# Products of zeros ahead of every four sums of squares, and the modulation of the next k tile inside a_v for k 1 to 8

## The chip, the core and the metric

The kernel runs on one core of one Trainium2 chip. A core has five engines with a queue of their own each: TensorE (PE, matrix products; the profile shows its weight loads apart, as PEld), VectorE (DVE), ScalarE (ACT), GpSimd (POOL) and SyncE (SP, which issues the DMAs here). Each works its queue off in order and waits on semaphores for the others. The metric is the device time of one execution in microseconds (us).

## What is computed

A trunk of two layers over 256 latent tokens and 256 context tokens of width 2048, all in float32. What matters here is how a layer begins:

```python
shift, scale, gate = jnp.split(silu_c @ w_mod[l] + b_mod[l], 3, axis=-1)
shift_c, scale_c, gate_c = jnp.split(silu_cc @ w_mod[l] + b_mod[l], 3, axis=-1)
h = rmsnorm(x, g_pre[l]) * (1.0 + scale[:, None]) + shift[:, None]
h_c = rmsnorm(ctx, g_pre[l]) * (1.0 + scale_c) + shift_c
proj = h @ w_in[l]
proj_c = h_c @ w_in[l]
```

`rmsnorm` divides each token by the root of the mean of its 2048 squares. `proj` is split by columns into nine parts: a_u, a_v, a_g (a gated MLP), b_q, b_k, b_v, b_g (attention) and c_x, c_g (a Fourier mixer). The branches' outputs are joined, go through an output projection and a second rmsnorm, and are added to the stream.

## The kernel before

**Layout.** The 2048 channels are 16 k tiles of 128 partitions. Latent and context tokens stand side by side, 512 columns: `yo[k]` holds x (later other things), `hh[k]` and `hl[k]` the high and the low part of h. A product of two float32 matrices is made of three products of such parts (`mm3`, L405 to L408). A float32 product that isn't split (`ps_mod`, `ps_rs`) shows as two records in the trace.

**The order.** PE's queue is written out by hand for the whole kernel. While the first stage lasts (until k 14 of layer 0's loop, L626) the queues of DVE, ACT and SP are in the order of the code too; after it a scheduler orders these.

**The prologue** (L1132 to L1173). SP issues the 16 x tiles, 256 KB each, then two small tables, the modulation weights of k tile 0 (four loads of 512 KB, L167: tiles `mraw` twice, `macc`, `vv`), a projection weight (`raw`, L365), the modulation weights of k tile 1 (`mg`, `mgl`, `hh`/`hl`), a projection weight, and so on. For each x tile ACT squares it into one of seven `w2k` buffers (L1144), one of which the first small table holds meanwhile, and PE sums it over the partitions by a product with ones (L1147). The sum for tile k goes to 32 of the 128 columns of the array, by k % 4:

```python
c = slice(32 * (k % 4), 32 * (k % 4) + 32)
PE.matmul(sq[c], ones[:, 0:32], q, start=k < 4, stop=k >= KT - 4, tile_position=(0, 32 * (k % 4)))
```

`warm(ps, n)` (L448 to L451) puts n products of zeros (`wz`, bfloat16, 128 x 512) into a PSUM bank that nobody reads yet; ahead of each sum stands one. After the sums, copies on ACT, small products, a power on GpSimd and a broadcast give `rb0`, one over the root mean square of each token.

**The modulation of a k tile** (`mod_start`, L151 to L192) is 16 products of the 16 blocks of SiLU(c), SiLU(c_ctx) with 128 columns each of scale and shift, in four groups (`kg`), four column groups of 32 in each. The generator stops after each group, so the caller places the groups. Then DVE transposes the result (L175), a small product sums four quarters (`ps_modc`, L180), and DVE adds the bias (L189 to L192). Each group's weights are loaded when its products are put in the queue; a load waits for its buffer, which the products of the k tile two before have used.

**Layer 0's opening loop** (L598 to L660). For each k it accumulates a_v (four token tiles, `start_av`, 12 products) and the first three heads of a_u (`start_au`, three products a head). Meanwhile the modulation of tile k + 1 is computed (`mods_next`, all four groups, then `LOADS[k]` loads of projection weights into three `raw` buffers), and with it `h_next` makes hh, hl of k + 1: DVE multiplies (L484), ACT adds the shift and rounds (L488), DVE makes the low part (L493). `h_next` also splits `SPLITS[k]` projection weights into high and low (ACT L384, DVE L386), which frees their raw buffers. Where the four modulation groups stand on PE:

| k | order on PE |
| --- | --- |
| 0 | a_v, groups, products of zeros, a_u |
| 1, 2 (`k < MIDDLE`) | a_v, a_u head 0, groups, a_u head 1, modc; k 2 then a_u head 2 for k 0 to 2 |
| 3, 4 | half of a_v, groups, other half, modc, a_u |
| 5 to 15 (`k >= NEXT`) | groups, a_v, modc, a_u |

`W` (L332 to L401) streams the projection weights; `take` asks it for the next tile. After the loop the other parts of the projection follow as products over all 16 k tiles (`tunit`, `ps_t`).

Of the kernel before, what the change touches and what calls it, by code (L numbers as in the profile page):

```python
# [66 lines left out]
def trunk_kernel(ctx: ExitStack, tc: tile.TileContext, xT, xhalf, cT, wss, wsl, wmod, win, wout0, wout1, const, vec, rows,  # L67
# [9 lines left out]
    def sb(shape, dt, tag, bufs=1):  # L77
        cnt[0] += 1
        return pool.tile(shape, dt, tag=tag, bufs=bufs, name=f"{tag}_{cnt[0]}")

    def w2k(shape, dt=F32):
        return sb(shape, dt, "w2k", W2K)

    def mm_ps(name="mm"):
        cnt[0] += 1
        return psum.tile([P, 512], F32, tag="mm", bufs=6, name=f"ps_{name}_{cnt[0]}")

    def ms_ps(name="ms"):
        cnt[0] += 1
        return psum.tile([P, 512], F32, tag="ms", bufs=2, name=f"ps_{name}_{cnt[0]}")  # L90
# [29 lines left out]
    def cc(name):  # L120
        o, w = COFF[name]
        return cst[:, o - P:o - P + w]
# [154 lines left out]

    LOADS = [1, 1, 1, 2, 1, 1, 1, 1, 1, 0, 2, 0, 1, 1, 1, 0]
    SPLITS = [1, 1, 1, 2, 0, 1, 0, 2, 1, 1, 0, 2, 0, 1, 1, 1]
    MIDDLE, NEXT = 3, 5  # L280
    LOWC = 60
    YT = 3.0
    GATES = {4: 0}, {0: 1}, {0: 2, 14: 3}, {}
# [48 lines left out]
    class Stream:  # L332
# [64 lines left out]
        def next(self):  # L397
            self.fetch()
            pace()
            self.pos += 1  # L400
            return self.out[self.pos - 1]  # L401
# [3 lines left out]
    def mm3(ps, st, mv, start, stop):  # L405
        PE.matmul(ps, st[0], mv[0], start=start, stop=False)  # L406
        PE.matmul(ps, st[0], mv[1], start=False, stop=False)  # L407
        PE.matmul(ps, st[1], mv[0], start=False, stop=stop)  # L408

    def part(w, c):  # L410

        def of(t):
            if not isinstance(t, list):
                return t[:, c]
            n = t[0].shape[-1]
            return t[c.start // n][:, c.start % n:c.start % n + c.stop - c.start]

        return of(w[0]), of(w[1])
# [29 lines left out]
    def warm(ps, n):  # L448

        for _ in range(n):  # L450
            PE.matmul(ps, wz[:, 0:P], wz, start=True, stop=True)  # L451
# [16 lines left out]
    def h_of(l, k, sl):  # L468

        if l == 0:  # L470
            return hh[k][:, sl], hl[k][:, sl]
        s, a = sl.start // S, sl.start % S
        t, b = (hh, hl)[s][k], a + sl.stop - sl.start
        return t[:, a:b], t[:, S + a:S + b]

    def make_h(l, k, rb, streams, between=()):

        if streams[0] == 0:
            new_h(k)
        t = w2k([P, T])  # L480
        for s in streams:
            sl = slice(s * S, (s + 1) * S)
            rsl = slice((s - streams[0]) * S, (s - streams[0] + 1) * S)
            V.scalar_tensor_tensor(out=t[:, sl], in0=yo[k][:, sl], scalar=gs[l][:, k, s:s + 1],  # L484
                                   in1=rb[:, rsl], op0=ALU.mult, op1=ALU.mult)
        for s in streams:
            sl = slice(s * S, (s + 1) * S)
            first = A.activation(h_of(l, k, sl)[0], t[:, sl], AF.Identity, bias=sh[l][:, k, s:s + 1])  # L488
        next(iter(between), None)
        for s in streams:  # L490
            sl = slice(s * S, (s + 1) * S)
            hi, lo = h_of(l, k, sl)
            last = V.scalar_tensor_tensor(out=lo, in0=t[:, sl], scalar=sh[l][:, k, s:s + 1],  # L493
                                          in1=hi.bitcast(F32), op0=ALU.add, op1=ALU.subtract)
        return first, last
# [58 lines left out]
    def layer(l):  # L554
        last = l == 1
        n = S if last else T
        nt = n // P
# [11 lines left out]
        au = [mm_ps("au") for _ in range(2)] + [ms_ps("au") for _ in range(1 - l)]  # L569
# [3 lines left out]
        def take(k, which=(0,)):  # L573

            for i in which:
                if k % (2, 4, 8)[i] == 0:
                    ws_[i] = W.next()

        def start_av(k, ts):
            avw = ws_[0]  # L580
            c = slice((k % 2) * 512, (k % 2 + 1) * 512)
            for t in ts:
                sl = slice(t * P, (t + 1) * P)
                mm3(av[t], h_of(l, k, sl), part(avw, c), k == 0, k == KT - 1)
# [13 lines left out]
        if l == 0:  # L598
            for k in range(KT):
                m = mod_start(k + 1, 1) if k + 1 < KT else iter([None] * 4)  # L600

                def mods_next():
                    for _ in range(4):
                        next(m)
                    for _ in range(LOADS[k]):
                        W.load()

                def h_next():

                    todo = SPLITS[k]  # L610
                    if k + 1 < KT:
                        list(m)
                        e = W.emitting(512) if todo else iter(())
                        next(e, None)
                        make_h(0, k + 1, rb0, [0, 1], e)
                        list(e)
                        todo -= todo > 0
                    for _ in range(todo):
                        W.emit()

                if k % 2 == 0:
                    take(k)
                if k >= NEXT:
                    mods_next()
                    start_av(k, range(nt))
                    if k == KT - 2:  # L626
                        first_stage.close()
                    h_next()
                    if k >= KT - 2:
                        for _ in range(2):  # L630
                            with low(LAG), tc.issue_after(W.last.ins):
                                next(mods)
                    take(k, (1, 2))
                    start_au(k)
                elif k == 0:
                    start_av(0, range(nt))
                    mods_next()
                    warm(au[2], 3)
                    h_next()
                    warm(au[2], 6)  # L640
                    take(0, (1,))
                    start_au(0, (0, 1))
                elif k < MIDDLE:
                    start_av(k, range(nt))
                    take(k, (1,))
                    start_au(k, (0,))
                    mods_next()
                    start_au(k, (1,))
                    h_next()
                    if k == 2:  # L650
                        ws_[2] = W.next()
                        for i in range(k + 1):
                            start_au(i, (2,))
                else:
                    start_av(k, range(nt // 2))
                    mods_next()
                    start_av(k, range(nt // 2, nt))
                    h_next()
                    take(k, (1,))
                    start_au(k)  # L660
        for i, (k0, nk) in enumerate(blocks if l else ()):
            for k in range(k0, k0 + nk):
# [466 lines left out]
    with tc.manual_schedule(engines={EN.PE}):  # L1129

        first_stage.enter_context(tc.manual_schedule(engines={EN.DVE, EN.Activation, EN.SP}))
        DMA.dma_start(ct, cT)  # L1132
        for k in range(KT):
            DMA.dma_start(yo[k], xT[k])
        raw = w2k([P, NFIRST])
        DMA.dma_start(raw, const[:, 0:NFIRST])
        DMA.dma_start(vecs, vec)
        V.memset(wz, 0.0)
        A.activation(cs, ct, AF.Silu)
        V.tensor_copy(cpad[:, :, 0:2], cs)  # L1140
        sq, idle = mm_ps("rs2"), mm_ps("idle")
        for k in range(KT):
            q = w2k([P, T])
            A.activation(q, yo[k], AF.Square)  # L1144
            warm(idle, 1)
            c = slice(32 * (k % 4), 32 * (k % 4) + 32)
            PE.matmul(sq[c], ones[:, 0:32], q, start=k < 4, stop=k >= KT - 4, tile_position=(0, 32 * (k % 4)))  # L1147
        A.copy(identr, raw[:, 0:P])
        A.copy(cst[:, 0:NFIRST - P], raw[:, P:])
        row = w2k([P, T])  # L1150
        A.copy(row, sq)
        m = mod_start(0, 1)
        next(m)
        warm(idle, 2)
        ps = ms_ps("rs")
        for j in range(4):
            PE.matmul(ps[:, j:j + 1], row[:, j * P:(j + 1) * P], cc("sel")[:, 0:1], start=True, stop=True)
        r0 = rstd_cols(ps[:, 0:4], 4, D)
        next(m)
        warm(idle, 2)  # L1160
        rb = bcast(r0, 4)
        rb0 = sb([P, T], F32, "acc")
        A.copy(rb0, rb)
        next(m)
        next(m)
        W.load()
        warm(idle, 3)
        list(m)
        warm(idle, 4)
        e = W.emitting(512)  # L1170
        next(e)
        make_h(0, 0, rb0, [0, 1], e)
        list(e)  # L1173
        layer(0)
        state["acc"] = out_proj()
        layer(1)
        finish()

# [76 lines left out]
```

## Time and profile before

| what | value |
| --- | --- |
| time, median of 3 runs | 1166.96 us (1165.6 to 1167.47) |
| the profiled execution's own time | 1166.71 us |
| its span, first to last instruction | 1164.9 us |
| granted PE clock over the span | 0.996 |
| PE on the chain that ended last | 95% of the span |
| data moved | 234.30 MB, mean 201 GB/s |

The span is what the profile shows; the time has the launch around it. Rows of the timeline give start, duration, engine, line, operation, output<-inputs, shape and count; in brackets the time that the engine idled before the row, and what ended it. Such a row can merge several instructions. A record of a product lasts longer than the distance to the next, since products are pipelined.

### The profile page before, as it was taken

The page shows a single profiled execution, that of the slowest core. Times are in us where ns is not written, and L with a number is a line of the kernel's source. Part 1 is how long each engine was busy: PE and PEld are TensorE (multiplying, and loading weights), DVE is VectorE, ACT ScalarE, POOL GpSimd, SP SyncE. Part 2 cuts the span into 40 slices and gives each one's busy share as a digit, 9 for nine tenths or more (in the row PEclk, how much of TensorE's full clock was granted, in tenths as well). Part 3 has the DMA queues.
Part 4 walks back from the last instruction along what each step waited for, and adds up shares of the span by engine and source line. Part 5 has one row for each costly group of instructions (what it writes and reads, how often), then busy time and mean ns, then how long its engine had stood idle before and what let it go on. Part 6 is the DMA issues. An engine that isn't in the chain of part 4 may idle for free.

```text
span 1164.9 us, 17002 instructions
## 1 busy us (share of the span) xinstructions
PE 1144.4 (98%) x6383; PEld 936.5 (80%) x6386; DVE 881.2 (76%) x1504; ACT 522.1 (45%) x964; POOL 32.4 (3%) x39
## 2 busy tenths in 40 slices
PE   8999999999999999999999999999999999999996
PEld 1566678888889888888888888888888988888885
DVE  0344479989998788698999995376888679868775
ACT  4222252322233766642433233356665369856442
POOL 0000000000000000000000000200500000000001
PEclk9999999999999999999999999999999999999999
DMA  9797954556665343345656674355956665556873
GB/s 334 278 334 299 384 197 167 179 182 207 213 219 190 112 128 135 109 162 184 207 166 213 197 236 146 95 174 194 214 164 202 207 221 195 164 165 205 306 254 109
DMA packets 72227, 234.30 MB, mean 201 GB/s; under 512 B 8400, under 2 KB 11600, under 8 KB 72144
## 3 DMA queue, kind: packets, MB, share of 16 engines
q1 hardware_dynamic: 69840, 231.11, 59.1%
q0 software_dynamic: 2304, 2.10, 1.2%
q8 instruction: 50, 0.82, 0.3%
q14 instruction: 33, 0.27, 0.1%
HBM read 231.08 MB, written 2.10 MB: 200 GB/s over the span
## 4 chain that ended last, share of the span: by engine, by line
PE 95%; DVE 2%; DMA 1%; ACT 1%; issue 1%; POOL 0%; SPq 0%; DVEq 0%; POOLq 0%; ACTq 0%
PE ps_t L406 15%; PE ps_t L408 15%; PE ps_t L407 15%; PE ps_t L522 10%; PE ps_t L523 5%; PE ps_mod L170 2%; PE ps_y L407 2%; PE ps_y L408 2%; PE ps_y L406 2%; PE ps_av L406 2%; PE ps_av L407 2%; PE ps_av L408 2%; PE ps_tp L846 2%; PE ps_rs L1147 1%; PE ps_v L408 1%; PE ps_v L407 1%
## 5 line engine op out<-in xcount | busy, mean ns | idle before, releaser
L384 ACT CAST whi<-raw 128x1024 fp32r<-128x1024 f32 (+1 forms) x226 | 227.6, 1013 | 335.4 <-PE ps_t L407 223.1
L386 DVE TENSOR_TENSOR wlo<-raw,whi 128x1024 fp32r<-128x1024 f32 (+1 forms) x226 | 264.2, 1172 | 61.3 <-ACT whi L384 58.6
L406 PE MATMUL ps_t<-hh,whi 128*128 128x512 f32 (+1 forms) x768 | 294.3, 383 | 0.0
L408 PE MATMUL ps_t<-hh,wlo 128*128 128x512 f32 (+1 forms) x768 | 292.6, 381 | 0.0
L407 PE MATMUL ps_t<-hl,whi 128*128 128x512 f32 (+1 forms) x768 | 292.5, 381 | 0.0
L207 DVE SCALAR_TENSOR_TENSOR macc<-mraw,cs,macc 128x512 f32<-128x512 f32 x360 | 248.8, 744 | 14.9 <-DMA mraw<-in_wmod_dram 14.9
L522 PE MATMUL ps_t<-hh,whi 128*128 128x512 f32 x512 | 184.8, 399 | 0.0
L408 PEld LDWEIGHTS ps_t<-hh,wlo 128*128 128x128 f32 x768 | 144.4, 188 | 28.0
L406 PEld LDWEIGHTS ps_t<-hh,whi 128*128 128x128 f32 x768 | 144.4, 188 | 27.6 <-issue 1.5
L407 PEld LDWEIGHTS ps_t<-hl,whi 128*128 128x128 f32 x768 | 144.4, 188 | 26.2 <-issue 0.2
L523 PE MATMUL ps_t<-hh,wlo 128*128 128x256 f32 x512 | 143.4, 280 | 0.0
L522 PEld LDWEIGHTS ps_t<-hh,whi 128*128 128x128 f32 x512 | 96.1, 188 | 20.7 <-issue 0.2
L523 PEld LDWEIGHTS ps_t<-hh,wlo 128*128 128x128 f32 x512 | 96.8, 189 | 0.2 <-issue 0.2
L488 ACT ACTIVATE hh<-w2k,sh 128x256 fp32r<-128x256 f32 x48 | 21.8, 502 | 95.2 <-DVE w2k L484 95.2
L406 PE MATMUL ps_y<-whi,hh 128*128 128x512 f32 x112 | 46.0, 411 | 0.0
L407 PE MATMUL ps_y<-wlo,hh 128*128 128x512 f32 x112 | 43.7, 390 | 1.2 <-DVE tot L992 1.2
L408 PE MATMUL ps_y<-whi,hl 128*128 128x512 f32 x112 | 43.8, 391 | 0.0
L406 PE MATMUL ps_av<-whi,hh 128*128 128x512 f32 x96 | 40.0, 416 | 2.2 <-ACT hh L488 2.2
L407 PE MATMUL ps_av<-wlo,hh 128*128 128x512 f32 x96 | 38.6, 402 | 0.4 <-DVE wlo L386 0.4
L423 ACT CAST w2k<-ps_tp 128x512 fp32r<-128x512 f32 x40 | 23.4, 584 | 23.1 <-PE ps_scc L407 12.7
L175 DVE STREAM_TRANSPOSE w2k<-ps_mod 128x256 f32<-128x256 f32 x16 | 7.2, 449 | 34.1 <-PE ps_mod L170 30.7
L436 POOL TENSOR_TENSOR rs_b<-rs_a,mhalf 128x2 f32<-128x2 f32 (+1 forms) x7 | 7.3, 1041 | 811.7 <-DVE rs_a L434 811.7
(364 smaller groups left out, 1775.7 us busy)
## 6 DMA issues: line engine op xcount, KB each, us to landing
raw<-in_win_dram SPq DMA_DIRECT2D x160, 512.0 KB, 3.7
mraw<-in_wmod_dram SPq DMA_DIRECT2D x128, 512.0 KB, 4.2
raw<-in_wout_dram SPq DMA_DIRECT2D x64, 512.0 KB, 4.3
mraw<-in_wsl_dram SPq DMA_DIRECT2D x16, 512.0 KB, 5.8
yo<-in_xT_dram SPq DMA_DIRECT2D x16, 256.0 KB, 5.4
macc<-in_wsl_dram SPq DMA_DIRECT2D x8, 512.0 KB, 6.9
vv<-in_wsl_dram SPq DMA_DIRECT2D x8, 512.0 KB, 7.3
mg<-in_wsl_dram SPq DMA_DIRECT2D x8, 512.0 KB, 5.7
```

Of the source, the lines that this page charges most:

```text
L170: PE.matmul(ps[32 * kk:32 * kk + 32, 0:n], cpad[:, kg * 4 + kk], ws[kk], start=kg == 0, stop=kg == 3, tile_position=(0, 32 * kk))
L207: V.scalar_tensor_tensor(out=acc[:, s], in0=w[:, kk % 2], scalar=c, in1=acc[:, s], op0=ALU.mult, op1=ALU.add)
L384: A.copy(ph, r[:, c])
L386: self.last = V.tensor_tensor(out=pl, in0=r[:, c], in1=ph.bitcast(F32), op=ALU.subtract)
L406: PE.matmul(ps, st[0], mv[0], start=start, stop=False)
L407: PE.matmul(ps, st[0], mv[1], start=False, stop=False)
L408: PE.matmul(ps, st[1], mv[0], start=False, stop=stop)
L423: A.copy(hi, src)
L488: first = A.activation(h_of(l, k, sl)[0], t[:, sl], AF.Identity, bias=sh[l][:, k, s:s + 1])
L522: PE.matmul(ps, w[0], h, start=k == 0, stop=False)
L523: PE.matmul(ps[:, 0:S], w[1], h[:, 0:S], start=False, stop=k == KT - 1)
L846: PE.transpose(tp[:, (2 * j + b) * P:(2 * j + b + 1) * P], src, ident)
```

## The change

Three things. The prologue's single product of zeros ahead of each sum becomes six ahead of the sums of tiles 0, 4, 8 and 12, and none elsewhere (24 instead of 16). In k 1 and 2 two of the four modulation groups go to the middle of a_v and two behind it, a_u head 0 follows, then `h_next`, then a_u head 1, and in k 1 four products of zeros. `NEXT` goes from 5 to 9, so k 5 to 8 have all four groups in the middle of a_v, as k 3 and 4 have, and that branch's `take` can also ask for the weights of a_u head 2, which k 8 needs. The lines below the loop move down by 4 or 5.

```diff
-    MIDDLE, NEXT = 3, 5
+    MIDDLE, NEXT = 3, 9
...
-                def mods_next():
-                    for _ in range(4):
+                def mods_next(pieces=4, loads=True):
+                    for _ in range(pieces):
                         next(m)
-                    for _ in range(LOADS[k]):
+                    for _ in range(LOADS[k] if loads else 0):
                         W.load()
...
                 elif k < MIDDLE:
-                    start_av(k, range(nt))
+                    start_av(k, range(nt // 2))
+                    mods_next(2, False)
+                    start_av(k, range(nt // 2, nt))
+                    mods_next(2)
                     take(k, (1,))
                     start_au(k, (0,))
-                    mods_next()
+                    h_next()
                     start_au(k, (1,))
-                    h_next()
+                    if k == 1:
+                        warm(au[2], 4)
                     if k == 2:
                         ws_[2] = W.next()
                         for i in range(k + 1):
...
                     h_next()
-                    take(k, (1,))
+                    take(k, (1, 2))
                     start_au(k)
...
             A.activation(q, yo[k], AF.Square)
-            warm(idle, 1)
+            if k % 4 == 0:
+                warm(idle, 6)
             c = slice(32 * (k % 4), 32 * (k % 4) + 32)
```

## The prediction

> **What bounds the kernel now.** I read the page first, then the engines by stretch, then the opening instruction by instruction on TensorE (PE), ScalarE (ACT) and the DMA queue (SP).
>
> ```profile
> span 1164.9 us, 17002 instructions
> PE 1144.4 (98%) x6383; PEld 936.5 (80%) x6386; DVE 881.2 (76%) x1504; ACT 522.1 (45%) x964; POOL 32.4 (3%) x39
> ```
>
> PE works for 98% of the span, so whatever takes time away from PE's own queue, or fills its few gaps, moves the end by as much. The diff touches only the sums of squares and layer 0's opening loop over k; after that the PE program is the same in both kernels. Two stretches of the opening stand out.
>
> ```profile
> 15.00:20.00 5.00, 5.00 (x13) 0.93 (x12) 0.00 (x0) 2.44 (x5) 0.00 (x0) 1.00 1.03 409
> 50.00:60.00 10.00, 8.46 (x59) 5.33 (x58) 3.48 (x11) 1.94 (x4) 0.00 (x0) 0.83 0.89 312
> ```
>
> After the stretch come PE, PEld, DVE, ACT and POOL busy, the granted clock, the DMA share and GB/s. While the sums run (15 to 20 us is a part of it) PE is full and ACT is not; at 50 to 60 us PE idles and is granted 0.83 of its clock.
>
> **The sums of squares.** Today PE alternates one product of zeros (L451, all 128 columns) and one sum (L1147, 32 columns):
>
> ```profile
> 1.90 0.61 PE L451 MATMUL ps_idle<-join 128*128 128x512 bf16 x1 [1.90 <-DVE join L1138]
> 4.73 1.91 PE L1147 MATMUL ps_rs<-w2k,ones 128*32 128x512 f32 x2 [2.22 <-ACT w2k L1144]
> 9.28 1.04 PE L1147 MATMUL ps_rs<-w2k,ones 128*32 128x512 f32 x2
> 10.25 0.39 PE L451 MATMUL ps_idle<-join 128*128 128x512 bf16 x1
> 10.57 1.05 PE L1147 MATMUL ps_rs<-w2k,ones 128*32 128x512 f32 x2
> 26.60 0.59 PE L1147 MATMUL ps_rs<-w2k,ones 128*32 128x512 f32 x1
> ```
>
> From 9.28 on the pitch is 10.57 - 9.28 = 1.29 us a tile: 10.25 - 9.28 = 0.97 for the sum, 0.32 for the zeros. The last of 16 ends at 26.60 + 0.59 = 27.19. ACT could go faster; in the second half it waits for PE to give the buffers of the squares back:
>
> ```profile
> 4.04 0.63 ACT L1144 ACTIVATE w2k<-yo 128x512 f32<-128x512 f32 x1 [1.44 <-DMA yo<-in_xT_dram]
> 8.65 2.70 ACT L1144 ACTIVATE w2k<-yo 128x512 f32<-128x512 f32 x4 [0.57 <-DMA yo<-in_xT_dram]
> 11.66 0.63 ACT L1144 ACTIVATE w2k<-yo 128x512 f32<-128x512 f32 x1 [0.31 <-PE ps_rs L1147]
> ```
>
> The changed kernel puts six products of zeros ahead of tiles 0, 4, 8 and 12 and runs four sums back to back, each on its own 32 columns. The trace has no two sums in a row, so their price is bounded from two rows. The nearest is the modulation product (L170): same 32 columns, four column groups in a row, f32, half the columns streamed:
>
> ```profile
> 66.18 1.07 PE L170 MATMUL ps_mod<-mraw,kt 128*32 128x256 f32 x16
> 67.06 0.61 PE L170 MATMUL ps_mod<-macc,kt 128*32 128x256 f32 x8
> 68.04 0.50 PE L406 MATMUL ps_av<-whi,hh 128*128 128x512 f32 x1
> 32.40 0.82 PE L451 MATMUL ps_idle<-join 128*128 128x512 bf16 x3
> 41.19 1.47 PE L451 MATMUL ps_au<-join 128*128 128x512 bf16 x6
> ```
>
> Two records are one product. Eight products take 67.06 - 66.18 = 0.88 us, so four take 0.44, though one with half a sum's columns should need half of 0.97, some 0.49: the four column groups run beside each other. So four sums cost between 0.97 (all together) and 4 x 0.97 = 3.9 us. I take 0.97 from the moment the last of the four squares is there. Six products of zeros take 6 x 0.217 = 1.3 us ((1.47 - 0.82) / 3 each), 1.5 with the changes from and to 32 columns. Per four tiles that is 2.5 us of PE. ACT needs 4 x 0.675 = 2.7 (2.70 for four), and the transfers hardly less, so ACT and the transfers become the limit. The last x tile:
>
> ```profile
> 1.19 9.12 SPq L1134 DMA_DIRECT2D yo<-in_xT_dram  x16
> yo<-in_xT_dram SPq DMA_DIRECT2D x1, 256.0 KB, 5.4
> 14.05 0.33 SPq L167 DMA_DIRECT2D vv<-in_wsl_dram  x1
> vv<-in_wsl_dram SPq DMA_DIRECT2D x1, 512.0 KB, 7.0
> ```
>
> Its issue ends at 1.19 + 9.12 = 10.31 and starts 0.33 earlier, at 9.98; it lands 5.4 us later, at 15.4. Square: 16.05. Sum: 17.1. I checked that PE keeps up. The first six products of zeros run from 1.90, where PE waits for data anyway, 0.61 + 5 x 0.43 (0.43 being the 512-column pitch of the 0.5 clock, row below) to 4.7, and delay nothing. Then squares 3, 7, 11 and 15 end near 7.4, 10.7, 13.3 and 16.05, their sums near 8.4, 11.7, 14.4 and 17.1, with 1.5 us of zeros in each gap. (8.65 less the 0.57 idle is the end of square 4, one square earlier is 7.4; 10.7 is three squares into the four; 13.3 is 16.05 less four.) At the half clock the first group ends 0.9 later, which the next two make up. The wait for a group's last square is new; behind it stand only the next zeros, and nobody waits for those. The sums end **10.1 us** earlier.
>
> What is late next? From the sums to the first av product today:
>
> ```profile
> 35.05 0.49 PE L406 MATMUL ps_av<-whi,hh 128*128 128x512 f32 x1 [0.63 <-ACT hh L488]
> ```
>
> 35.05 - 27.19 = 7.86 us of copies, GpSimd and VectorE steps, unchanged; from 17.1 that gives 24.96. The last modulation weight of k tile 0 (vv) lands at 14.05 + 7.0 = 21.05; its four products (0.44) end when the three zeros of 32.40 start, so PE wants it at 31.95 - 10.1 = 21.85. The SP queue issues all this as before. So these loads stay hidden, by 0.8 us, and nothing is given back here.
>
> **k 1 and 2.** The mod products move into av in two pairs, and one au head moves behind them.
>
> ```profile
> 44.29 0.39 PE L406 MATMUL ps_av<-whi,hh 128*128 128x512 f32 x1
> 50.55 0.25 PE L180 MATMUL ps_modc<-w2k,cst 128*32 128x4 f32 x8
> 52.33 0.49 PE L406 MATMUL ps_av<-whi,hh 128*128 128x512 f32 x1 [1.53 <-ACT hh L488]
> 54.94 0.63 PE L406 MATMUL ps_av<-whi,hh 128*128 128x512 f32 x1
> 55.36 0.63 PE L407 MATMUL ps_av<-wlo,hh 128*128 128x512 f32 x1
> 57.19 0.39 PE L406 MATMUL ps_au<-hh,whi 128*128 128x512 f32 x1
> 60.73 0.24 PE L180 MATMUL ps_modc<-w2k,cst 128*32 128x4 f32 x8
> 62.96 0.50 PE L408 MATMUL ps_au<-hh,hh 128*128 128x512 f32 x1 [1.33 <-DVE hh L386]
> 64.70 0.40 PE L406 MATMUL ps_av<-whi,hh 128*128 128x512 f32 x1
> ```
>
> Today k 1 lasts 52.33 - 44.29 = 8.04 us, k 2 64.70 - 52.33 = 12.37. In k 1 the next h is ready 52.33 - 50.55 = 1.78 us after modc (L180), and PE idles 1.53 of it. After the gap, products come every 55.36 - 54.94 = 0.42 us instead of 0.23: the half clock.
>
> Changed, k 1 from its start, at 0.23 a product, 0.44 a mod group, 0.1 for each change of columns and 0.34 for the first product behind one: half av 1.46, two mod groups 0.98, half av 1.58, two groups 0.98, au head 0 0.88; modc at 5.88, h at 5.88 + 1.78 = 7.66. PE after modc: 0.17, au head 1 0.80, four products of zeros 0.9: busy until 7.8. The gap closes; k 1 lasts 7.8, **0.2** less. Were the h chain longer, up to the 1.53 of today would come back.
>
> k 2 at full clock: the third product needs VectorE's low half of h, as it comes 0.25 late, so modc is at 6.13. The wait for au2's low half ends 62.96 - 60.73 = 2.23 us after modc, at 8.36 (0.8 of it idle, 1.33 today), and the rest is 64.70 - 62.96 = 1.74: 10.1 in all, **2.3** less, mostly the slow clock (57.19 - 52.33 = 4.86 for 12 products that need 2.8). Their mod weights are there: with the sums shorter, the queue need not wait for PE to free buffers. Behind the x tiles (15.4) come two small tables (0.17 MB), three k tiles' mod weights and two projection loads, 14 x 0.524 MB: 7.5 MB, 18.4 us at the 409 GB/s of 15 to 20 us, so tile 2's weights are there at 33.8. PE starts k 1 at 44.29 - 10.1 = 34.2 and needs the first of them 1.5 us later.
>
> The slow clock after 1.53 us of gap is the trace's own evidence. [...]
>
> **k 5 to 8** take the form that k 3 and 4 have already.
>
> ```profile
> 71.97 0.39 PE L406 MATMUL ps_av<-whi,hh 128*128 128x512 f32 x1
> 79.37 1.07 PE L170 MATMUL ps_mod<-mraw,kt 128*32 128x256 f32 x16
> 86.62 0.64 PE L170 MATMUL ps_mod<-mg,kt 128*32 128x256 f32 x8
> ```
>
> k 3 in the new form lasts 71.97 - 64.70 = 7.27, k 5 in the old one 86.62 - 79.37 = 7.25: no change on PE, the groups only trade places. Their buffers come free 1.5 us later, and the loads of k + 2 that wait for them might too. The place where loads are tight is k 9:
>
> ```profile
> 102.28 0.33 SPq L365 DMA_DIRECT2D raw<-in_win_dram  x1
> 104.12 0.39 SPq L167 DMA_DIRECT2D vv<-in_wsl_dram  x1
> 110.96 0.64 PE L170 MATMUL ps_mod<-vv,kt 128*32 128x256 f32 x8 [0.64 <-DMA vv<-in_wsl_dram]
> 104.00:124.00 20.00, 19.34 (x148) 12.65 (x146) 9.10 (x27) 4.39 (x10) 0.00 (x0) 1.00 1.02 402
> ```
>
> vv for k tile 10 is issued behind raw, which waits for the splits of k 7, not for the mod buffer: k 7 starts at 79.37 + 2 x 7.25 = 93.9 and has used that buffer by 95.7, changed by 97.2, both well ahead of 102.28. modc, and so the splits, stand where they stood in k 7. The 0.64 stays, all else shifts along. In the SP queue one load moves, the tables for the later branches (0.39 MB, 1.0 us at 402 GB/s), from ahead of that raw to behind the loop's last one; nothing waits for it in the loop. ACT takes the GELUs at the loop's end in another order. Cost 0 for all of these; what they could cost or gain is some tenths, inside the range.
>
> **Sum:** 10.1 + 0.2 + 2.3 = 12.6 us. The profiled execution took 1166.71 (1.8 around its span), the median of the three runs is 1166.96. 1166.7 - 12.6 = **1154.1**.
>
> **Rivals.**
> - The slow stretch stays (the clock falls for another reason, or k 2's 0.8 us gap is enough): k 2 keeps 2.0 of its loss, 1156.1. [...] Against: the row of 52.33.
> - The four sums don't overlap, so the change doesn't do what it says. Then the first four end at 4.73 + 2 x 1.91 + 2 x 0.97 = 10.5, each further four takes 3.9 + 1.4 = 5.3, and the sums end at 26.4, 0.8 early: 1166.7 - 0.8 - 2.5 = 1163.4. Against: 0.44 us for four mod products.
> - Slower: the stream of loads becomes the bound of the whole loop. Then the 12.6 us reappear as PE waits for mod weights, and the later release of buffers in k 5 to 8 costs 4 x 1.46 = 5.8 more: 1172.5. It decides once one k tile's loads (2.1 MB of modulation and about 0.5 of projection weights) take more than PE's 7.25 us, below 360 GB/s. For it: the 402 GB/s without a pause behind k 8, and the 0.64 wait. Against: 2.6 MB at 402 take 6.5 us.
>
> **How the numbers follow.** Forecast 0.74, slow stretch 0.11, no overlap 0.10, loads 0.05. The forecast's own spread is 1151.5 (a gap-free k 2, 0.8 and 0.64 gained, and an earlier last sum) to 1156; with the slow stretch at up to 1158.5 the range holds 0.85. About 0.2% (2.3 us) is what a measurement can tell from no change: faster 0.93 (forecast, slow stretch, most of no overlap), same 0.02, slower 0.05.
>
> **What would show it.** Right: four sums starting as their squares end, the last ending near 17; first av near 25; ACT's waits for PE gone from the squares; no granted clock below 1.00 between 40 and 60 us; k 2 near 42, k 3 near 52, k 5 near 66.7; the vv wait at k 9 still 0.6. Wrong: sums 0.97 apart, a longer list of DMA waits on L170, or a shift that shrinks between k 3 and the end of the loop.

## The result, and the profile after

The changed kernel takes 1155.33 us (median of 4 runs, 1154.37 to 1156.34), the kernel before in the same sessions 1166.47: ratio 0.9904, 95% interval 0.9887 to 0.9921. That is 11.1 us less; the forecast was 12.6 less, 1154.1. The profiled execution of the changed kernel took 1155.36 us.

The head of the page of the changed kernel:

```profile
span 1153.6 us, 17028 instructions
PE 1136.7 (99%) x6394; PEld 935.3 (81%) x6398; DVE 880.7 (76%) x1504; ACT 522.1 (45%) x964; POOL 33.3 (3%) x39
```

The span is 11.3 us shorter, PE's busy time 7.7 us. Two stretches of the same table as before (busy time of PE, PEld, DVE, ACT, POOL, then granted clock, DMA share, GB/s):

```profile
15.00:20.00 5.00, 4.75 (x39) 2.18 (x38) 0.16 (x1) 2.32 (x6) 0.01 (x1) 1.00 1.02 410
50.00:60.00 10.00, 9.36 (x70) 6.29 (x69) 4.81 (x14) 2.56 (x6) 0.00 (x0) 1.00 0.88 312
```

At 15 to 20 us the sums end and the modulation begins; the clock at 50 to 60 us is 1.00. PE's timeline of the prologue in the changed kernel (start, duration, instruction, count, idle time before):

```profile
1.90 2.74 PE L451 MATMUL ps_idle<-join 128*128 128x512 bf16 x6 [1.90 <-DVE join L1142]
4.66 2.28 PE L1152 MATMUL ps_rs<-w2k,ones 128*32 128x512 f32 x4
7.72 1.71 PE L1152 MATMUL ps_rs<-w2k,ones 128*32 128x512 f32 x4 [0.78 <-ACT w2k L1148]
9.37 1.47 PE L451 MATMUL ps_idle<-join 128*128 128x512 bf16 x6
10.76 1.44 PE L1152 MATMUL ps_rs<-w2k,ones 128*32 128x512 f32 x8
13.53 1.38 PE L1152 MATMUL ps_rs<-w2k,ones 128*32 128x512 f32 x8
16.24 1.41 PE L1152 MATMUL ps_rs<-w2k,ones 128*32 128x512 f32 x8
17.74 0.64 PE L170 MATMUL ps_mod<-mraw,kt 128*32 128x256 f32 x8
25.80 0.49 PE L406 MATMUL ps_av<-whi,hh 128*128 128x512 f32 x1 [0.63 <-ACT hh L488]
```

Four sums (eight records) take 1.4 us instead of 4 x 0.97 = 3.9, the groups follow each other every 2.7 us, and the last sum ends at 16.24 + 1.41 = 17.65, before at 27.19. ACT now squares without waiting for PE, as its timeline shows (the 14 last squares in one row):

```profile
7.04 9.51 ACT L1148 ACTIVATE w2k<-yo 128x512 f32<-128x512 f32 x14 [1.56 <-DMA yo<-in_xT_dram]
```

The starts of k 1, 2 and 3, modc and the stall of k 2, and the wait at k 9, again on PE's timeline:

```profile
35.06 0.40 PE L406 MATMUL ps_av<-whi,hh 128*128 128x512 f32 x1
42.81 0.50 PE L406 MATMUL ps_av<-whi,hh 128*128 128x512 f32 x1
49.28 0.24 PE L180 MATMUL ps_modc<-w2k,cst 128*32 128x4 f32 x8
51.52 0.50 PE L408 MATMUL ps_au<-hh,hh 128*128 128x512 f32 x1 [0.64 <-DVE hh L386]
53.24 0.39 PE L406 MATMUL ps_av<-whi,hh 128*128 128x512 f32 x1
99.45 0.64 PE L170 MATMUL ps_mod<-vv,kt 128*32 128x256 f32 x8 [0.64 <-DMA vv<-in_wsl_dram]
```

k 1 lasts 42.81 - 35.06 = 7.75 us (8.04 before), k 2 53.24 - 42.81 = 10.43 (12.37). By the start of k 3 the changed kernel leads by 64.70 - 53.24 = 11.46 us, and at the end of the span by 11.3.

### The profile page after: what moved, and what is told of

The parts are those of the page before. It is cut to its first block, busy times and chain, and to the rows that moved or that the text cites. A ratio compares the mean times of both kernels' runs of the same rounds, so it can differ in the third digit from the quotient of the medians.

```text
span 1153.6 us, 17028 instructions
## 1 busy us (share of the span) xinstructions
PE 1136.7 (99%) x6394; PEld 935.3 (81%) x6398; DVE 880.7 (76%) x1504; ACT 522.1 (45%) x964; POOL 33.3 (3%) x39
## 4 chain that ended last, share of the span: by engine, by line
PE 87%; DMA 6%; DVE 5%; issue 1%; ACT 1%; SPq 0%; POOL 0%; DVEq 0%; ACTq 0%; POOLq 0%
PE ps_t L406 15%; PE ps_t L408 15%; PE ps_t L407 15%; PE ps_t L522 10%; PE ps_t L523 5%; PE ps_mod L170 2%; DMA mraw<-in_wmod_dram 2%; PE ps_av L406 2%; PE ps_av L407 2%; PE ps_av L408 2%; DVE wlo L386 2%; PE ps_tp L850 2%; PE ps_v L408 1%; PE ps_v L407 1%; PE ps_v L406 1%
## 5 line engine op out<-in xcount | busy, mean ns | idle before, releaser
L386 DVE TENSOR_TENSOR wlo<-raw,whi 128x1024 fp32r<-128x1024 f32 (+1 forms) x226 | 264.7, 1174 | 55.6 <-ACT whi L384 53.0
```

What stands on the lines that cost most here:

```text
L386: self.last = V.tensor_tensor(out=pl, in0=r[:, c], in1=ph.bitcast(F32), op=ALU.subtract)
```

## The experiments

The theory: the sums gain because four of them run beside each other on different column groups; the loop gains because the gap in k 1 no longer lowers the clock. Rivals: the sums gain because there are fewer changes between products of 128 and of 32 columns; the slow stretch came from something else than the gap. Each run has its own comparison with the kernel before on the same chip (medians of 1167.0 to 1167.4 us there).

**The sums alone** (the diff is against the kernel before).

```diff
-            warm(idle, 1)
+            if k % 4 == 0:
+                warm(idle, 6)
```

> The kernel before, with only the sums of squares changed (six products of zeros ahead of tiles 0, 4, 8 and 12). If the four sums overlap on their column groups, the sums end near 17.6 us (before 27.2), the first av product starts near 25.8 (before 35.05), and the time is about 9.2 us below before, near 1157.3; k 1 and 2 together keep their 20.4 us (8.04 + 12.37), or some 2 us less if the slow clock stays away. If the gain of the changed kernel came from the loop instead, the time is near 1164.

Measured: 1155.93 us, ratio 0.9898 (0.9879 to 0.9916), 11.4 us less and so 2.2 more than expected; the changed kernel's ratio of 0.9904 lies within this interval. The sums bring nearly all of it. PE's timeline of this run:

```profile
14.98 1.46 PE L1148 MATMUL ps_rs<-w2k,ones 128*32 128x512 f32 x8
24.57 0.49 PE L406 MATMUL ps_av<-whi,hh 128*128 128x512 f32 x1 [0.63 <-ACT hh L488]
41.85 0.51 PE L406 MATMUL ps_av<-whi,hh 128*128 128x512 f32 x1 [1.54 <-ACT hh L488]
```

The sums end at 16.44, the first av product starts at 24.57. The gap of k 1 is there, 1.54 us (1.53 in the kernel before), but no slow stretch follows (stretches of this run; PE, PEld, DVE, ACT, POOL, then the clock):

```profile
37.59:41.00 3.41, 2.72 (x43) 1.39 (x35) 1.04 (x5) 0.00 (x0) 0.00 (x0) 1.00 1.05 399
41.00:44.42 3.42, 2.57 (x10) 1.80 (x10) 2.64 (x6) 1.94 (x4) 0.00 (x0) 1.00 1.03 411
44.42:47.83 3.41, 3.41 (x40) 1.98 (x38) 0.00 (x0) 0.00 (x0) 0.00 (x0) 1.00 1.01 404
```

k 2 lasts 10.74 us here with the old loop and its gap. So the gap doesn't always lower the clock, and this part of the theory is taken up again below.

**k 1 and 2 alone**: the new loop form for k 1 and 2, with the old sums and the old NEXT (the diff is against the changed kernel).

```diff
-    MIDDLE, NEXT = 3, 9
+    MIDDLE, NEXT = 3, 5
...
-            if k % 4 == 0:
-                warm(idle, 6)
+            warm(idle, 1)
```

> The changed kernel with the sums of squares as before (one product of zeros ahead of each) and NEXT back at 5: only k 1 and 2 in the new form. The step of the prediction: k 1 lasts 7.8 and k 2 10.4 instead of 8.04 and 12.37, no granted clock below 1.00 between 40 and 70 us, the time 2.2 us below before, near 1164.3. If the slow stretch came from something other than the gap, k 2 stays above 12 us and the time is within 0.7 us of before.

Measured: 1165.40 us, ratio 0.9984 (0.9975 to 0.9993), 2.0 us less than its before. k 1 lasts 7.74 and k 2 10.43, as in the changed kernel, with products 0.23 us apart in both.

**Four sums on the same columns**, otherwise the changed kernel.

```diff
-            c = slice(32 * (k % 4), 32 * (k % 4) + 32)
-            PE.matmul(sq[c], ones[:, 0:32], q, start=k < 4, stop=k >= KT - 4, tile_position=(0, 32 * (k % 4)))
+            c = slice(32 * (k // 4), 32 * (k // 4) + 32)
+            PE.matmul(sq[c], ones[:, 0:32], q, start=k % 4 == 0, stop=k % 4 == 3, tile_position=(0, 32 * (k // 4)))
```

> The changed kernel, but four sums in a row go to the same 32 columns (group k // 4 instead of k % 4): as many products of zeros and as many changes between 128 and 32 columns, no neighbours on different column groups. If the overlap of column groups makes the gain, the sums follow each other 0.86 to 0.97 apart, end near 25 to 26 us, and the time is near 1163. If the gain came from fewer changes between the two widths, the sums end below 20 us and the time stays near 1155.

Measured: 1161.76 us, ratio 0.9948 (0.9933 to 0.9964). PE's timeline:

```profile
4.57 4.95 PE L1152 MATMUL ps_rs<-w2k,ones 128*32 128x512 f32 x8
10.84 3.62 PE L1152 MATMUL ps_rs<-w2k,ones 128*32 128x512 f32 x8
15.79 3.62 PE L1152 MATMUL ps_rs<-w2k,ones 128*32 128x512 f32 x8
22.92 1.45 PE L1152 MATMUL ps_rs<-w2k,ones 128*32 128x512 f32 x3
```

Four sums take 3.6 us instead of 1.4, and the last ends at 24.37. With the same zeros and the same changes of width, 17.65 turns into 24.37: the overlap is worth 6.7 us, and only 27.19 - 24.37 = 2.8 us come from the rest. Of these, 2.1 stand behind the first four sums already (they end at 4.57 + 4.95 = 9.52, before at 10.57 + 1.05 = 11.62): their zeros now run while PE waits for the first squares. The rival falls as the main cause. Nor is it that sums into the same place wait for each other: one takes 0.9 us here and 0.97 in the kernel before, where one sum and the next go to different places.

**Zeros in the gap of k 1 of the kernel before.**

```diff
                     start_au(k, (1,))
                     h_next()
+                    if k == 1:
+                        warm(au[2], 6)
```

> The kernel before, with six products of zeros (1.3 us) behind the making of h in k 1, where PE idled 1.53 us; nothing else. If the gap lets the clock fall, the granted clock stays 1.00 at 50 to 60 us, k 2 lasts near 10.4 instead of 12.37, and the time is about 1.9 us below before. [...]

Measured: 1165.88 us, ratio 0.9978 (0.9967 to 0.9989), 1.5 less than its before. k 2 lasts 10.79, with products 0.23 us apart, where the half clock of before had 0.42. (The profiled execution is the slowest of the ten, 1169.41; the others took 1164.82 to 1166.9.)

**NEXT alone**, in the kernel before.

```diff
-    MIDDLE, NEXT = 3, 5
+    MIDDLE, NEXT = 3, 9
...
-                    take(k, (1,))
+                    take(k, (1, 2))
```

> The kernel before with only NEXT at 9 (k 5 to 8 with the modulation groups in the middle of a_v). The step of the prediction: each k still lasts 7.25 to 7.27 us, the wait for vv at k 9 stays at 0.6, the time is that of before within 0.3 us. If the later release of the buffers of the modulation weights counts, the wait for vv grows to 2 us or more and the time rises by as much.

Measured: 1167.60 us, ratio 1.0002 (0.9994 to 1.0011), and the wait for vv is 0.6: k 5 to 8 cost and gain nothing. This profile, too, has k 1's gap of 1.54 us without a slow stretch behind it (products every 0.23 us); k 2 lasts 10.72.

**No products of zeros in k 1**, otherwise the changed kernel.

```diff
-                    if k == 1:
-                        warm(au[2], 4)
```

> The changed kernel without the four products of zeros in k 1. The next h is ready 1.78 us after modc, so PE idles about 0.8 us ahead of k 2 and k 1 lasts 7.66 instead of 7.75. If a gap of 0.8 us with the stall of 0.64 in k 2 is enough to lower the clock, the granted clock falls for one stretch of 3.4 us and the time rises by 1.5 to 2 us; if it takes the 1.5 us of before, the time is the changed kernel's within 0.2 us, and the four products buy nothing.

Measured: 1154.56 us, ratio 0.9888 (0.9873 to 0.9903). PE idles 0.65 us there, the products behind it come every 0.23 us, k 1 and 2 last 7.74 and 10.44. The four products buy nothing; moving au head 1 behind modc had already shortened the gap.

**No products of zeros between the sums**, otherwise the changed kernel.

```diff
-            if k % 4 == 0:
+            if k == 0:
                 warm(idle, 6)
```

> The changed kernel with six products of zeros ahead of tile 0 only, none ahead of tiles 4, 8 and 12. [...] If the zeros held the sums up, the sums end earlier than 17.3.

Measured: 1154.97 us, ratio 0.9894 (0.988 to 0.9908). All 16 sums (32 records) stand in one row of PE's timeline:

```profile
4.59 12.06 PE L1152 MATMUL ps_rs<-w2k,ones 128*32 128x512 f32 x32
```

They end at 16.65, and the granted clock over the span is 0.997 here and 0.998 in the three other runs, in the changed kernel 0.998 in all four. The transfers and ACT set the pace, and the zeros between cost nothing and buy nothing. (PE's records show it busy throughout: in the kernel before one sum takes 0.97 us, and ACT has the next square ready after some 0.67.)

**Where does a gap lower the clock?** The granted clock changed on a grid of 3.413 us: in the profiled execution of the kernel before it fell to 0.50 at 53.33 us, rose again at 56.75, and fell once more at 1159.24, 324 such cells behind 53.33. The origin differs from run to run (a border of the run below is 52.77). In the kernel before, the whole gap (50.79 to 52.33) lay inside one cell (49.92 to 53.33), and the next cell ran at 0.5; in the sums-alone run two cells shared the gap (2.72 and 2.57 us of work in the rows above) and the clock stayed at 1.00. A kernel with more such gaps tells this apart: the kernel before, with k 3 to 7 in the form of k 1.

```diff
-    MIDDLE, NEXT = 3, 5
+    MIDDLE, NEXT = 8, 8
...
-                    start_au(k, (0,))
+                    start_au(k, (0,) if k < 3 else (0, 2))
                     mods_next()
                     start_au(k, (1,))
                     h_next()
```

> The kernel before, with k 3 to 7 in the form of k 1 (heads 0 and 2 of a_u, the groups, head 1, then the gap), so that up to six gaps of about 1.5 us lie at different places of the 3.413 us grid on which the granted clock changed in the profiles so far. Theory: the clock is lowered for one cell of the grid when at least 1.5 us of the cell before were idle, and not at 1.34 or less; a gap that two cells share does nothing. So some of the gaps, about half, are each followed by 3.4 us at 0.5, and which ones can be told from their place. [...] The time rises by 7 to 11 us through the gaps and the slow stretches.

Measured: 1183.04 us in one execution, 16 above before: more than expected, since loads at the later k also waited. Five gaps of 1.54 us came about. Cells of the grid in this run (PE busy, granted clock, DMA share, GB/s):

```profile
49.36:52.77 3.41, 1.87 (x17) 1.00 0.65 213
52.77:56.18 3.41, 3.41 (x9) 0.50 0.99 382
80.08:83.49 3.41, 1.99 (x31) 1.00 0.77 264
83.49:86.90 3.41, 3.30 (x14) 1.00 0.97 350
86.90:90.32 3.42, 3.42 (x40) 1.00 0.47 175
100.56:103.97 3.41, 1.87 (x18) 1.00 0.91 329
103.97:107.38 3.41, 3.41 (x10) 0.50 1.01 369
121.04:124.45 3.41, 1.65 (x24) 1.00 1.03 422
124.45:127.87 3.42, 3.12 (x13) 0.50 1.03 393
```

A cell with 1.87 us of work (1.54 idle) is followed by one at 0.50, at 49.36, 69.84 and 100.56. The gap from 82.06 to 83.60 ends 0.11 us behind a border: 1.99 us of work (1.42 idle), and the clock stays. The last two cells hold no such gap: there three waits for modulation weights (0.77 us, 0.64, and 0.36 of the third's 0.66) leave 1.65 us of work, and the next cell runs at 0.50 too. So 1.54 us of idle time can be enough, but not every gap of 1.54 us lowers the clock.

**Two splits one k tile earlier**, in the changed kernel, against the two stalls that are left in the loop.

```diff
-    SPLITS = [1, 1, 1, 2, 0, 1, 0, 2, 1, 1, 0, 2, 0, 1, 1, 1]
+    SPLITS = [1, 2, 0, 2, 0, 1, 1, 1, 1, 1, 0, 2, 0, 1, 1, 1]
```

> The changed kernel with two splits of projection weights one k tile earlier (the list SPLITS begins 1, 2, 0, 2, 0, 1, 1, 1 instead of 1, 1, 1, 2, 0, 1, 0, 2): au2's first weights in k 1 and tile 7 in k 6. Expected: the wait of 0.64 us for au2's low half in k 2 goes, and raw of tile 10 and the modulation weights of k tile 10 are issued one k tile (7 us) earlier, so the wait of 0.64 us for vv at k 9 goes too: 1.3 us below the changed kernel, near 1154.0. If another wait takes their place (a projection weight, or transfers that are now late at k 11), less than 0.4 us is left.

Measured: 1158.96 us, ratio 0.9929 (0.9915 to 0.9944): 3 to 4 us slower than the changed kernel, where 1.3 less was expected. k 2 did shorten to 9.49, but PE now waits for modulation weights at k 9, 11 and 13. Two of these rows:

```profile
98.64 0.64 PE L170 MATMUL ps_mod<-macc,kt 128*32 128x256 f32 x8 [0.59 <-DMA macc<-in_wsl_dram]
99.94 0.64 PE L170 MATMUL ps_mod<-vv,kt 128*32 128x256 f32 x8 [0.65 <-DMA vv<-in_wsl_dram]
```

The split of tile 3 came ahead of its load, so the program loaded it out of turn, and every later load of a projection tile moved one place ahead in the SP queue. There each waits for a split of one k tile later, with the modulation weights behind it: from 40 to 145 us SP waits 44.6 us ahead of loads of projection weights for the low part of a split (DVE, L386), in the changed kernel 29.0. The next run moves that load along with its split:

```diff
-    LOADS = [1, 1, 1, 2, 1, 1, 1, 1, 1, 0, 2, 0, 1, 1, 1, 0]
-    SPLITS = [1, 1, 1, 2, 0, 1, 0, 2, 1, 1, 0, 2, 0, 1, 1, 1]
+    LOADS = [1, 2, 0, 2, 1, 1, 1, 1, 1, 0, 2, 0, 1, 1, 1, 0]
+    SPLITS = [1, 2, 0, 2, 0, 1, 1, 1, 1, 1, 0, 2, 0, 1, 1, 1]
```

> The changed kernel with the two earlier splits of the run before this one (SPLITS begins 1, 2, 0, 2, 0, 1, 1, 1), and the load of tile 3 moved with its split (LOADS begins 1, 2, 0, 2), so that the loads of the later projection tiles keep their places. If the earlier run lost its time because one split came ahead of its load and all later loads moved by one place, then here k 2 lasts near 9.5 us (10.43 in the changed kernel), the wait for vv at k 9 is gone, and the time is 1.3 to 1.6 us below the changed kernel, near 0.9877 of before. If the earlier splits themselves are too much for ACT and VectorE, waits on L170 or L406 remain and the time is not below the changed kernel's.

Measured: 1152.67 us (1152.35 to 1154.25), ratio 0.9872 (0.9852 to 0.9892), where 0.9877 was expected. In the medians it is 2.7 us faster than the changed kernel, but the two intervals overlap. In the profile k 2 lasts 9.49 us, and from the first av product to the end of the loop PE has one wait left, the one ahead of that first product:

```profile
PE ps_av L406 <- ACT hh L488: 0.6, 1, 0.6
```

The waits for vv and for au2's low half are gone. Not all of the 3.0 us between the two profiles comes from this: the first av product starts at 24.87 here and at 25.80 in the changed kernel, ahead of anything that the edit touches.

## Why the prediction was right, and where it wasn't

The sign, the place and nearly the size held: 12.6 us forecast, 11.3 between the two spans, 11.1 between the medians.

- **The sums** (10.1 forecast): 27.19 - 17.65 = 9.5 in the profiles, 27.19 - 16.44 = 10.75 in the sums-alone run. The pace is that of the x tiles and of ACT, as the step said; in the changed kernel's profiled execution the third x tile came late (ACT idled 1.56 us ahead of 7.04) and with it the last square, at 16.55 instead of 16.05. That was this execution: in the five other runs with four sums in a row on different columns the first av product starts between 24.57 and 24.97, where 24.96 was forecast. The overlap, taken from the modulation rows, is shown by the run on the same columns; its price as a rival, 1163.4, was 1.6 above what that run took.
- **From the sums to the first av product**, taken as unchanged: 8.15 us (25.80 - 17.65) instead of 7.86. PE's timeline of the kernel before has the reason, rows that the prediction had not used:

```profile
26.15 0.62 PE L1147 MATMUL ps_rs<-w2k,ones 128*32 128x512 f32 x1
26.15 0.63 PE L170 MATMUL ps_mod<-mraw,kt 128*32 128x256 f32 x6
```

The first modulation products ran beside the last sum, on the columns that it left free; these rows alone show products of two kinds overlap. Now that group comes after the sums and costs 0.3 us of the chain.
- **k 1** (0.2): 0.29. **k 2** (2.3): 1.94 between the profiles. Its modc came 49.28 - 42.81 = 6.47 after its start instead of 6.13, since the halves of h and of the weights that VectorE makes hold up the first products by more than the 0.25 taken; the step from modc to au2 was 51.52 - 49.28 = 2.24, as forecast.
- **The step that failed is the cause given for most of these 2.3 us**: "After the gap, products come every 55.36 - 54.94 = 0.42 us instead of 0.23: the half clock." That was read as what this gap always does; in the runs it went with the place on the grid (inside one cell 0.50 in the next, at 49.92 in before and three times in the run with more gaps; across a border 1.00, at 82.06 to 83.60). Without a slow stretch k 2 of the old form lasts 10.72 to 10.79 (sums alone, NEXT alone, zeros in the gap), so 12.37 - 10.74 = 1.6 us of k 2 belong to the stretch that the profiled execution of before happened to have. The new form itself gains 0.3 in k 1 and 0.3 in k 2. That the two profiles differ by 11.3 us, near the 12.6 forecast, is thus partly luck: with a profile of before that had no stretch there, they would have differed by some 9.7 (an estimate, 11.3 - 1.6).
- **What closing the gap is worth in the mean.** A gap of 1.54 us lies within one cell of 3.41 in (3.41 - 1.54) / 3.41 = 55% of places; if all places were alike, closing it would be worth 0.9 us more in the mean (an estimate). The runs show more. Zeros in the gap alone gained 1.5 us in the medians, with an interval of 1.3 to 3.9 (its ratios, times 1167.36) that leaves out 0.9. And the granted clock over the span is 0.9960 in the mean of the 43 runs of the kernel before that list it, 0.9960 in the ten of NEXT alone and 0.9965 in the four of the sums alone, which all have the gap, but 0.9976 in the ten with zeros in it and 0.9980 in the ten with k 1 and 2 alone. 0.0016 of 1166 us is 1.9 us of lost clock, and one stretch loses half of 3.41, 1.7. So the gap costs about one stretch an execution (an estimate from these two numbers), though two of the four profiles with the gap (sums alone, NEXT alone) show none at k 2. Why it is more than the places give stays open.
- **k 5 to 8 at no cost, and the 0.64 us at k 9 unchanged**: right (ratio 1.0002; 0.64 at 99.45). The slower rival, loads as the bound of the loop, didn't come: after the start of k 3 only 64.70 - 53.24 - 11.3 = 0.2 us of the lead were given back. The run with two splits earlier shows the sign that was named for it, DMA waits on L170, but there the loads waited for splits, which is another cause.
- **The products of zeros**, which the prediction counted as free, are free, and the 18 between the sums and the four in k 1 are also without use (1154.97 and 1154.56 us without them, 1155.33 with all); no run leaves out the six ahead of the first sum.

## What to carry to other kernels

Products that use 32 columns each ran beside each other here when neighbours in PE's queue were on different column groups (four sums in 1.4 us), not when they were on the same columns (3.6 us) and not with a product of full width between them (4 x 0.97 = 3.9 us), so put such fillers around groups and not into them. The price of a stall in one profile may not hold in the next: k 1's gap was followed by a k 2 of 12.37 us in the profile of before, and of 10.74 and 10.72 in two other runs that have it. Look at a second execution before such a price goes into a sum. A split or load moved to an earlier place has to take everything along that the queue counts on, or all that stands behind it waits for another event (1158.96 us without the load, 1152.67 with it).

## What the runs showed of the hardware

The granted clock of PE changed on the borders of cells of 3.413 us: at 53.33, 56.75 and 1159.24 in the kernel before, at 52.77, 73.25, 103.97 and 124.45 (6, 15 and 21 cells behind the first) in the run with more gaps. Six cells of three profiles, with 1.53 us or more idle, were followed by one at 0.50: 49.92 in the kernel before (1.88 us of work, 1.53 idle), 49.36, 69.84 and 100.56 (1.54 idle each) and 121.04 (1.76) in the run with more gaps, and one near the end of the run with NEXT alone (1.66, below). Two cells with 1.42 and 1.33 idle were followed by 1.00: 80.08 in the run with more gaps, and 60.16 to 63.57 in the kernel before (2.08 us of work). Idle time can't be the whole measure: behind PE's last product in the run with loads and splits moved, a cell with 1.57 idle was followed by 1.00 (columns PE busy, clock, DMA share, GB/s), though the cell of 49.36 above, with 1.87 us of work, was followed by 0.50:

```profile
1140.39:1143.80 3.41, 1.84 (x8) 1.00 0.62 231
1143.80:1147.22 3.42, 0.00 (x0) 1.00 0.34 117
```

The work in it is products of full width in a row, while the cells that brought 0.5 in the loop hold modulation products too; whether that makes the difference was not tested. The idle time need not be one gap: at 121.04 it was three (0.77, 0.64 and 0.36 us). Another cell with 1.5 us or more idle stands near the end of the run with NEXT alone (PE, PEld, DVE, ACT, POOL, then the clock, DMA share, GB/s):

```profile
1133.79:1137.21 3.42, 3.03 (x14) 2.18 (x12) 1.63 (x2) 2.71 (x6) 0.00 (x0) 1.00 0.40 146
1137.21:1140.62 3.41, 1.75 (x6) 1.24 (x7) 3.38 (x9) 1.89 (x4) 0.00 (x0) 1.00 0.59 167
1140.62:1144.03 3.41, 3.41 (x9) 2.67 (x8) 1.75 (x3) 1.83 (x4) 0.00 (x0) 0.50 0.41 141
```

Work of 1.75 us in the second cell, then 0.50. That execution was the slowest of its ten, 1169.13 against 1165.94 to 1168.08, so a part of the spread of a kernel's runs may come from such stretches (an estimate: one loses half of 3.41 us, 1.7). And with nothing between the 16 sums, of which ACT delivers one every 0.67 us, the granted clock over the span was 0.997 to 0.998 in four runs.
